# Projections over four PSUM banks, zeroing behind the last norm, and two loads and stores moved to ScalarE's queue

## The chip, the cores and the metric

One core of one Trainium2 chip runs the whole program; the other cores are idle. The metric is the device time of one execution in microseconds (us). Lower is better.

## What is computed

A two-layer model on 512 tokens of width 1024, in float32. Each layer is

```
h = rms_norm(x) ; proj = h @ w_in                       # 1024 -> 1024 + 968 + 1536 columns
mixed = concat(retention(4 heads), dsa(4 heads), dilated(8 heads))
x = x + mixed @ w_out
h = rms_norm(x) ; x = x + square(relu(h @ w_up)) @ w_down   # 1024 -> 4096 -> 1024
```

and a last `rms_norm` gives the output. `dsa` scores every key with an indexer of 8 heads, keeps the top keys of each query, and attends to those. `dilated` attends over three window patterns. `retention` runs in chunks of 128 tokens with a carried state.

## The kernel before

**Tiling.** Tokens are four tiles of 128 (t = 0 to 3). Every large product is made of three float32r matmuls (high·high, high·low, low·high), so each activation and each weight unit is kept as a high and a low half: ScalarE casts the high half, VectorE or GpSimd subtracts to get the low one (`prep`, L278 and L286, for weights; `norm`, L399 and L400, for activations). Weight units come through three raw buffers, loaded by DMA from SyncE's queue (`dma`, L263), into five unit buffers.

**PSUM.** Eight banks in three pools: `mm` has 2 (projections, output product, up product), `at` has 4 (transposes, scores, attention output), `rt` has 2 (retention; also the second half of a `dil_v` before retention begins). A new tile of a pool waits until the readers of the oldest one are done.

**Start.** `start()` loads a row of norm weights and two halves of token tile 2, spreads the row over 128 partitions with two matmuls (L1075), and then `norm` runs for tiles 2, 3, 0, 1. A norm squares the tile on ScalarE (L361), adds two sums on VectorE (L364), raises to the power -0.5 on GpSimd (L368, which gives the factor `r`), scales on VectorE (L387 and L389), transposes on TensorE (L352) and splits into halves (L399, L400). The first product is `token_parts` (L553, 456 columns, 96 matmuls for the four tiles).

**Attention.** The indexer (L336 with 384 columns), then top-k: 16 rounds of `max` and `match_replace` for three query tiles (L602, L603), in between the projections of the dilated heads: `proj` (L791) makes one q or k of a pair of heads in one `mm` bank, and `evac_q` and `evac_k` read it on ScalarE and on VectorE (L424, L438). `dil_v` makes the values. A head is `softmax` (L443, L444 for the scores, L462 for mask and minimum) and `attn_v` (transposes, L486 for the low half, L491). Retention steps go between the heads from head 5 on. `zeros()` (L814) fills the state `sv` and the unused halves of the two key buffers `KL` with zeros, five GpSimd instructions per layer.

**Order.** The code is handed to a scheduler that orders each engine's instructions by priorities (table `PR`) and by its own idea of when things are ready. The order on an engine is then fixed; an instruction that waits holds up all behind it on its engine.

**End.** `final(t)` scales the last norm: one half of the columns on ScalarE (L1054), the other on VectorE (L1057). Both halves are stored from SyncE's queue (L1055, L1058).

Of the kernel before, what the change touches and what calls it, by code (L numbers as in the profile page):

```python
# [21 lines left out]
ALU = mybir.AluOpType  # L22
# [3 lines left out]
P = 128  # L26
# [25 lines left out]
C = {  # L52
    'FILL': 'q1,q2 k1 k2,g0,d g1,k3,q3 r,v s0,w,s1,',
    'RET': (0, 0, 0, 0, 0, 4, 0, 3, 0, 1, 3, 1, 0),
    'TOPK': (1, 1, 0, 4, 0, 10, 0),
    'POOL_LO': ('dv', 'o', 'sq', 'rg', 'rqk', 'dq', 'dk', 'ukv'),
    'LSPLIT': 2,
    'HOLD': 6,
    'KS': ((4, 6), (0, 2)),
    'SK': 1,  # L60
# [58 lines left out]
def bc(ap, dims):  # L119

    return bass.AP(ap.tensor, ap.offset, [list(ap.ap[0])] + [list(d) for d in dims])


class Kern:
# [251 lines left out]
    def norm(self, t, wb, act, room, first=False, h0=0):  # L376

        nc = self.nc
        hn = self.t(room[0], [P, 2, S], F32, room[1])
        halves = ((0, 512), (512, 1024))[::1 - 2 * h0]  # L380
        if not first:
            c0, c1 = halves[0]
            nc.gpsimd.tensor_tensor(hn[:, h0], self.x[t][:, c0:c1], wb[:, c0:c1], op=ALU.mult)
        r = self.norm_stats(t, None, halves)
        for h in (h0, 1 - h0):
            if h == h0 and not first:
                nc.vector.tensor_scalar(hn[:, h], hn[:, h], r[:, 0:1], None, op0=ALU.mult)  # L387
            else:
                nc.vector.scalar_tensor_tensor(hn[:, h], self.x[t][:, h * 512:(h + 1) * 512], r[:, 0:1],  # L389
                                               wb[h] if first else wb[:, h * 512:(h + 1) * 512], op0=ALU.mult,  # L390
                                               op1=ALU.mult)
            ps = self.at()
            for k in range(4):
                self.tr(ps[:, k * P:(k + 1) * P], hn[:, h, k * P:(k + 1) * P])
            psv = ps.rearrange("p (k c) -> p k c", k=4)
            for g in range(2):
                dst = act[h * 2 + g]
                hi = dst[:, 0, :, t * P:(t + 1) * P]
                nc.scalar.copy(hi, psv[:, 2 * g:2 * g + 2])  # L399
                nc.vector.tensor_tensor(dst[:, 1, :, t * P:(t + 1) * P], psv[:, 2 * g:2 * g + 2], hi.bitcast(F32),  # L400
                                        op=ALU.subtract)
# [135 lines left out]
    def dil_v(self, L, act, g):  # L537
        us = [(self.unit((L, "dv", g, k)), (k, k + 1, k + 2, k + 3)) for k in (0, 4)]
        for t in range(NT):
            ps = self.mm() if t < 2 else self.rt_bank()  # L540
            self.tform(us, act, t, ps, 256)
            self.evac_dil(ps[:, 0:256], g, t)
        self.done(2)
# [238 lines left out]
    def latent_k(self, L, pr):  # L782
# [5 lines left out]
            self.done()  # L788
        return self.evac_k(ps)

    def proj(self, key, act, cols=P):  # L791
        ps = self.mm()
        self.wform(self.unit(key), act, cols, ps, cols)
        self.done()
        return ps
# [17 lines left out]

    def zeros(self):  # L814

        z = lambda o, a: self.nc.gpsimd.tensor_scalar(o, a, 0.0, 0.0, op0=ALU.mult, op1=ALU.add)
        z(self.sv.rearrange("p a c -> p (a c)"), bc(self.ident, [[0, 4], [1, P]]))
        for i in range(4):
            o = slice(64, 128) if i % 2 == 0 else slice(0, 64)
            z(self.kl[i // 2][o, i % 2, :], bc(self.ident[o], [[0, 4], [1, P]]))  # L820

    def load_x(self, t, src):
        self.x[t] = self.t(self.pv, [P, D], F32, "xv")
# [6 lines left out]
    def attention(self, L, act):  # L830
        nc = self.nc
        A = self.A
        sc = None
        self.rt = [self.t(self.pmix, [P, 2, 1024], F32, "mix") for _ in range(2)]
        self.vd, self.sg, self.ct, self.vs, self.rqk_done = {}, None, None, None, False
        self.masks = self.t(self.psc, [P, N_CST - N_C1], F32, "masks")
        nc.sync.dma_start(self.masks, A["cst"][:, N_C1:])
# [54 lines left out]
        def out_part(h, t, ks, last=False):  # L892
            ps = self.mm()
            self.tform([(self.unit((L, "o", h, k)), (k, k + 1)) for k in ks], mix, t, ps)
            self.add_x(t, h, ps)
# [4 lines left out]
        for h in range(12 + C["SK"]):  # L900
            if h < 12:
                if h == 8:
                    self.bias(sc)
                with self.prio("hs", h):
                    self.head_s(heads[h // 2], h % 2)
            for f in fill.pop(0) if fill else ():
                with self.prio("fill", f):
                    steps[f]()
            if h == 8 + C["SK"]:
                for t in range(NT):  # L910
                    self.load_x(t, self.xd if L else A["x"])
                mix = [m0, None] + self.md
            if h >= 8 + C["SK"]:
                for _ in range(C["WO"]):
                    if wo and wo[0] not in hold:
                        assert 0 not in C["KS"][0] or m0_done
                        with self.prio("wo", h):
                            out_part(*wo.pop(0), C["KS"][0])
                            if wo and wo[0] == (1, 0):
                                self.done(len(C["KS"][0]))  # L920
            if h >= C["SK"]:
                with self.prio("hv", h):
                    self.head_v(heads[(h - C["SK"]) // 2], (h - C["SK"]) % 2)
            for _ in range(C["RET"][h] if h < 13 else 0):
                with self.prio("ret", h):
                    next(rets, None)
            if h < 6:
                with self.prio("topk", h):
                    self.topk(sc, C["TOPK"][h + 1])
# [117 lines left out]
    def final(self, t, wb, pool, junk):  # L1047
        nc = self.nc
        halves = [(512, 1024), (0, 512)]
        (c0, c1), (d0, d1) = halves  # L1050
        xs = self.t(pool, [P, 512], F32, "s")
        nc.gpsimd.tensor_tensor(xs, self.x[t][:, c0:c1], wb[:, c0:c1], op=ALU.mult)
        r = self.norm_stats(t, junk, halves if t != 1 else halves[:1] + [(d0, d0 + 256), (d0 + 256, d1)])
        nc.scalar.activation(xs, xs, AF.Copy, scale=r[:, 0:1])  # L1054
        nc.sync.dma_start(self.out[t * P:(t + 1) * P, c0:c1], xs)  # L1055
        o = self.x[t][:, d0:d1]
        nc.vector.scalar_tensor_tensor(o, o, r[:, 0:1], wb[:, d0:d1], op0=ALU.mult, op1=ALU.mult)  # L1057
        nc.sync.dma_start(self.out[t * P:(t + 1) * P, d0:d1], o)  # L1058

    def start(self):  # L1060
        nc = self.nc

        row = self.t(self.pt, [P, 2 * S], F32, "PT")
        nc.sync.dma_start(row[0:1, :], self.A["attn_norm_w"][0].rearrange("(o c) -> o c", o=1))
        self.x[2] = self.t(self.pv, [P, D], F32, "xv")
        for h in range(2):
            nc.sync.dma_start(self.x[2][:, h * 512:(h + 1) * 512], self.A["x"][2 * P:3 * P, h * 512:(h + 1) * 512])
        nc.sync.dma_start(self.c[:, :N_C0], self.A["cst"][:, :N_C0])
        nc.vector.memset(self.pwr, -0.5)
        one = self.work()  # L1070
        nc.vector.memset(one, 1.0)
        wps = [self.at(), self.at()]
        wb = self.t(self.ph, [P, D], F32, "ph")
        for h in range(2):
            nc.tensor.matmul(wps[h], one[0:1, 0:P], row[0:1, h * 512:(h + 1) * 512], start=True, stop=True)  # L1075
        for h in range(2):
            nc.scalar.copy(wb[:, h * 512:(h + 1) * 512], wps[h])
        self.plan()
        self.dma()
        self.load_x(3, self.A["x"])  # L1080
        self.dma()
        self.dma()
        self.load_x(0, self.A["x"])
        self.load_x(1, self.A["x"])
        nc.sync.dma_start(self.c[:, N_C0:], self.A["cst"][:, N_C0:N_C1])
        act = self.act_tiles()
        PRE = (1, 1, 2, 1)
        for t, n in zip((2, 3, 0, 1), PRE):
            self.norm(t, wps if t == 2 else wb, act, (self.pk, "KH" if t < 2 else "Q"), t == 2)
            self.done(n)  # L1090
        return act
# [38 lines left out]
```

## Time and profile before

| | us |
|---|---|
| median of 3 runs | 1236.36 (1236.02 to 1240.37) |
| profiled execution, its own time | 1236.08 |
| its span | 1234.1 |
| TensorE matmul busy | 1207.2 (98%) |
| VectorE busy | 921.4 (75%) |
| ScalarE busy | 679.2 (55%) |
| GpSimd busy | 472.4 (38%) |

How to read it: the span is what the profiler saw between the first and the last instruction; the profiled execution took 2.0 us more than that. Busy times are sums over the whole span, so they do not tell which engine sets the pace of a stretch. In rows of a timeline the columns are start, duration, engine, line, operation, output <- input, how many instructions were merged, and in brackets the idle time before and what ended it.

### The profile page before, as it was taken

How to read it: one execution, taken by the hardware profiler on the slowest of the kernel's cores; microseconds unless marked ns; L12 is line 12 of the kernel's file. 1: busy time of each engine (PE TensorE's matmuls, PEld its weight loads, DVE VectorE, ACT ScalarE, POOL GpSimd, SP SyncE). 2: the span in 40 equal slices, each digit the busy share in tenths (PEclk: the TensorE clock that was granted, in tenths of full speed). 3: DMA queues.
4: the chain of work that ended last, by engine and by line, in shares of the span. 5: the costliest groups of instructions: out<-in, count | busy, mean ns of one | idle time of the engine just before them, and what ended most of it. 6: DMA issues, size and time to landing. Idle time of an engine off the chain costs nothing.

```text
span 1234.1 us, 16904 instructions
## 1 busy us (share of the span) xinstructions
PE 1207.2 (98%) x6116; PEld 1027.6 (83%) x6116; DVE 921.4 (75%) x1582; ACT 679.2 (55%) x1241; POOL 472.4 (38%) x461
## 2 busy tenths in 40 slices
PE   7999999999999999999999999999999999999997
PEld 5988888889888888888889888888898888888886
DVE  5599957776875966858866997687769668587596
ACT  6645758745644535535566456686465354354454
POOL 3453748553412304214224546664534032140232
PEclk9999999999999999999999999999999999999999
DMA  7432324215244061260153323231180622514201
GB/s 217 120 83 72 95 69 121 86 53 188 85 137 137 1 215 58 69 184 16 35 166 102 95 71 96 91 120 53 52 256 1 205 68 69 176 30 140 82 1 69
DMA packets 142180, 122.73 MB, mean 99 GB/s; under 512 B 6801, under 2 KB 114065, under 8 KB 142098
## 3 DMA queue, kind: packets, MB, share of 16 engines
q1 hardware_dynamic: 140178, 118.52, 31.9%
q10 hardware_dynamic: 1920, 3.15, 1.0%
q8 instruction: 48, 0.79, 0.3%
q14 instruction: 34, 0.28, 0.1%
HBM read 114.31 MB, written 4.19 MB: 96 GB/s over the span
## 4 chain that ended last, share of the span: by engine, by line
PE 85%; DVE 12%; ACT 1%; issue 1%; DMA 1%; SPq 0%; POOL 0%; POOLq 0%; DVEq 0%; ACTq 0%
PE mm L336 35%; PE mm L348 15%; PE rt L1036 14%; PE at L1036 7%; PE mm L1036 3%; DVE sc L603 3%; DVE top L602 3%; PE at L352 2%; PE at L491 2%; PE at L444 1%; PE at L443 1%; DVE ph L462 1%; PE at L336 1%; DVE Q L424 1%; DMA raw<-in_w_in_dram 1%
## 5 line engine op out<-in xcount | busy, mean ns | idle before, releaser
L336 PE MATMUL mm<-act,w 128*128 128x512 f32 (+2 forms) x2352 | 516.1, 377 | 3.1 <-DVE Q L424 3.1
L336 PEld LDWEIGHTS mm<-act,w 128*128 128x128 f32 x2352 | 424.4, 188 | 79.8 <-issue 3.9
L286 POOL TENSOR_TENSOR w<-raw,w 128x512 fp32r<-128x512 f32 (+1 forms) x124 | 160.0, 1313 | 99.2 <-ACT w L278 74.0
L278 ACT CAST w<-raw 128x1024 fp32r<-128x1024 f32 (+1 forms) x138 | 142.9, 1037 | 79.2 <-PE rt L1036 27.6
L1036 PE MATMUL rt<-w,U 128*128 128x512 f32 x768 | 183.2, 389 | 0.0
L286 DVE TENSOR_TENSOR w<-rd,w 128x1024 fp32r<-128x1024 f32 x112 | 144.7, 1304 | 50.0 <-ACT w L278 50.0
L286 DVE TENSOR_TENSOR w<-raw,w 128x1024 fp32r<-128x1024 f32 (+1 forms) x76 | 94.0, 1238 | 107.5 <-ACT w L278 107.2
L1036 PEld LDWEIGHTS rt<-w,U 128*128 128x128 f32 x768 | 144.1, 188 | 29.9
L993 POOL TENSOR_TENSOR st<-s 128x256 f32<-128x256 f32 x32 | 39.1, 1223 | 330.1 <-ACT s L982 325.3
L278 ACT CAST w<-rd 128x1024 fp32r<-128x1024 f32 x112 | 117.6, 1050 | 83.4 <-PE rt L1036 41.7
L348 PE MATMUL mm<-w,act 128*128 128x456 f32 (+2 forms) x576 | 118.4, 351 | 3.0 <-DVE act L400 1.8
L348 PEld LDWEIGHTS mm<-w,act 128*128 128x128 f32 x576 | 96.4, 189 | 15.2 <-DVE act L400 2.8
L348 PE MATMUL mm<-w,mix 128*128 128x512 f32 x384 | 97.3, 401 | 0.6 <-DVE Q L424 0.5
L1036 PE MATMUL at<-w,U 128*128 128x512 f32 (+1 forms) x396 | 97.7, 386 | 0.0
L304 DVE TENSOR_TENSOR rd<-rd,rd 128x1024 f32<-128x1024 f32 x64 | 94.3, 1473 | 0.5
L1036 PEld LDWEIGHTS at<-w,U 128*128 128x128 f32 x396 | 73.6, 188 | 15.0
L980 ACT ACTIVATE s<-mm 128x512 f32<-128x512 f32 x62 | 36.9, 595 | 84.2 <-PE mm L336 74.5
L348 PEld LDWEIGHTS mm<-w,mix 128*128 128x128 f32 x384 | 70.5, 190 | 15.2 <-DVE Q L424 0.9
L997 ACT CAST U<-st 128x1024 fp32r<-128x1024 f32 x32 | 33.7, 1054 | 80.9 <-POOL st L994 80.9
L991 POOL TENSOR_TENSOR st<-s,s 128x256 f32<-128x256 f32 x32 | 36.7, 1146 | 92.0 <-ACT s L982 92.0
L463 ACT ACTIVATE ph<-ph,sm 128x128 f32<-128x128 f32 (+1 forms) x96 | 53.9, 562 | 24.5 <-DVE sm L462 23.8
L998 DVE TENSOR_TENSOR U<-s,U 128x256 fp32r<-128x256 f32 x64 | 63.9, 998 | 0.0
(169 smaller groups left out, 1766.4 us busy)
## 6 DMA issues: line engine op xcount, KB each, us to landing
raw<-in_w_up_dram SPq DMA_DIRECT2D x64, 512.0 KB, 4.2
rd<-in_w_down_dram SPq DMA_DIRECT2D x32, 1024.0 KB, 5.1
raw<-in_w_in_dram SPq DMA_DIRECT2D x48, 512.0 KB, 3.9
raw<-in_w_out_dram SPq DMA_DIRECT2D x16, 512.0 KB, 3.9
xv<-in_x_dram SPq DMA_DIRECT2D x7, 512.0 KB, 4.8
KH<-KH ACTq DMA_DIRECT2D x24, 128.0 KB, 2.3
raw<-in_w_in_dram SPq DMA_DIRECT2D x8, 256.0 KB, 2.9
xd<-xv SPq DMA_DIRECT2D x4, 512.0 KB, 3.9
```

Source lines behind the costliest of these rows:

```text
L278: self.nc.scalar.copy(hi, src)
L286: eng.tensor_tensor(lo[:, i:i + step], src[:, i:i + step], hi[:, i:i + step].bitcast(F32), op=ALU.subtract)
L304: sub = lambda o, a, b: self.nc.vector.tensor_tensor(o, a, b, op=ALU.subtract)
L336: self.nc.tensor.matmul(ps[:cols, toks[0]:toks[1]], a, b, start=(k == 0 and j == 0), stop=(k == KB - 1 and j == 2))
L348: self.nc.tensor.matmul(ps[:, :w], a, b, start=(n == 0), stop=(n == tot - 1))
L463: nc.scalar.activation(p, p, AF.Exp, bias=a, scale=-1.0, accum_out=b)
L602: nc.vector.max(m, sc[b])
L603: nc.vector.match_replace(sc[b], m, sc[b], SENT)
L980: nc.scalar.activation(s, ps, AF.Relu)
L993: tt(st[:, 2], a[:, 0], a[:, 1], op=ALU.subtract)
L998: nc.vector.tensor_tensor(lo, src, hi.bitcast(F32), op=ALU.subtract)
L1036: nc.tensor.matmul(ps[:, c0:c1], a, w, start=(new and n == 0), stop=(n == 11), skip_group_check=True)
```

## The change

Four edits. (1) Projections and `dil_v` take their bank from a new function `bank()`: two from `mm`, two from `rt`, in turn, until retention begins in the layer; after that from `mm` alone. (2) `zeros()` multiplies by the factor `r` of the last norm and by zero, so that it can run only once that norm's factor is there; in layer 0 that is the norm of tile 1 in `start()`, in layer 1 the last norm in the MLP of layer 0. (3) The row of norm weights is loaded from ScalarE's queue. (4) The ScalarE half of each output tile is stored from ScalarE's queue. The table of priorities is as it was.

```diff
@@ norm
         r = self.norm_stats(t, None, halves)
+        self.last_r = r
@@ dil_v
-            ps = self.mm() if t < 2 else self.rt_bank()
+            ps = self.bank()
@@ before proj
+    def bank(self):
+
+        self.nbank += 1
+        return self.rt_bank() if self.nbank % 4 in (3, 0) and not self.ret_started else self.mm()
+
     def proj(self, key, act, cols=P):
-        ps = self.mm()
+        ps = self.bank()
@@ zeros
-        z = lambda o, a: self.nc.gpsimd.tensor_scalar(o, a, 0.0, 0.0, op0=ALU.mult, op1=ALU.add)
+
+        z = lambda o, a, r=slice(0, P): self.nc.gpsimd.tensor_scalar(o, a, self.last_r[r, 0:1], 0.0, op0=ALU.mult,
+                                                                     op1=ALU.mult)
@@
-            z(self.kl[i // 2][o, i % 2, :], bc(self.ident[o], [[0, 4], [1, P]]))
+            z(self.kl[i // 2][o, i % 2, :], bc(self.ident[o], [[0, 4], [1, P]]), o)
@@ attention
+        self.nbank, self.ret_started = 0, False
@@
+            self.ret_started = self.ret_started or C["RET"][h] > 0
             for _ in range(C["RET"][h] if h < 13 else 0):
@@ final
-        nc.sync.dma_start(self.out[t * P:(t + 1) * P, c0:c1], xs)
+        nc.scalar.dma_start(self.out[t * P:(t + 1) * P, c0:c1], xs)
@@ start
-        nc.sync.dma_start(row[0:1, :], self.A["attn_norm_w"][0].rearrange("(o c) -> o c", o=1))
+        nc.scalar.dma_start(row[0:1, :], self.A["attn_norm_w"][0].rearrange("(o c) -> o c", o=1))
```

The lines of the changed kernel are 1 higher from L386 on, and 6 to 10 higher from L791 on.

**First place: the start.** GpSimd before, from its first work on data (`sv` and `KL` are zeroed, `sm` are the norms' small columns, 155, 193, 229 and 270 being the factors of tiles 2, 3, 0 and 1):

```order
L816 TENSOR_SCALAR sv_301<-cst 128x512
L816 TENSOR_SCALAR KL_63_302<-cst 64x512 x2
L816 TENSOR_SCALAR KL_64_303<-cst 64x512 x2
L368 TENSOR_TENSOR sm_155<-sm_149,pw 128x1
L383 TENSOR_TENSOR Q_184<-xv_128,ph_119 128x512
L368 TENSOR_TENSOR sm_193<-sm_187,pw 128x1
```

The five zeroing instructions stood ahead of the first factor; in the change they stand behind the fourth. VectorE at the start, before (`Q_147` is the scaled tile 2, `w_177`, `w_215`, `w_251` the first weight units, `act` the transposed halves):

```order
L364 SCALAR_TENSOR_TENSOR sm_149<-sm_148 128x1
L286 TENSOR_TENSOR w_177<-raw_124,w_177 128x912
L389 SCALAR_TENSOR_TENSOR Q_147<-xv_110,sm_155,at_117 128x512
L389 SCALAR_TENSOR_TENSOR Q_147<-xv_110,sm_155,at_118 128x512
L364 SCALAR_TENSOR_TENSOR sm_187<-sm_186 128x1
L286 TENSOR_TENSOR w_215<-raw_130,w_215 128x912
L387 TENSOR_SCALAR Q_184<-Q_184,sm_193 128x512
L389 SCALAR_TENSOR_TENSOR Q_184<-xv_128,sm_193,ph_119 128x512
L400 TENSOR_TENSOR act_143<-at_158,act_143 128x2x128
L286 TENSOR_TENSOR w_251<-raw_134,w_251 128x912
L364 SCALAR_TENSOR_TENSOR sm_223<-sm_222 128x1
L400 TENSOR_TENSOR act_144<-at_158,act_144 128x2x128
```

and in the change:

```order
L364 SCALAR_TENSOR_TENSOR sm_149<-sm_148 128x1
L390 SCALAR_TENSOR_TENSOR Q_147<-xv_110,sm_155,at_117 128x512
L286 TENSOR_TENSOR w_177<-raw_124,w_177 128x912
L390 SCALAR_TENSOR_TENSOR Q_147<-xv_110,sm_155,at_118 128x512
L364 SCALAR_TENSOR_TENSOR sm_187<-sm_186 128x1
L401 TENSOR_TENSOR act_143<-at_158,act_143 128x2x128
L388 TENSOR_SCALAR Q_184<-Q_184,sm_193 128x512
L390 SCALAR_TENSOR_TENSOR Q_184<-xv_128,sm_193,ph_119 128x512
L286 TENSOR_TENSOR w_215<-raw_130,w_215 128x912
L401 TENSOR_TENSOR act_144<-at_158,act_144 128x2x128
L401 TENSOR_TENSOR act_145<-at_168,act_145 128x2x128
L286 TENSOR_TENSOR w_251<-raw_134,w_251 128x912
```

The first half of tile 2 is scaled ahead of the first weight unit, and the halves `act_143`, `act_144` and `act_145` are split ahead of the third.

**Second place: the projections after the first k, in each layer.** TensorE before (911 is q of pair 0, 947 its k, 1014 q of pair 1, `at_987` the first head's scores, 1088 q of pair 2):

```order
L336 MATMUL mm_947<-act_146,w_649 128x512 x6
L336 MATMUL mm_1014<-act_143,w_721 128x512 x6
L336 MATMUL mm_1014<-act_144,w_721 128x512 x6
L336 MATMUL mm_1014<-act_145,w_721 128x512 x6
L336 MATMUL mm_1014<-act_146,w_721 128x512 x6
L443 MATMUL at_987<-KH_978,Q_942 128x128
```

and in the change:

```order
L336 MATMUL mm_947<-act_146,w_649 128x512 x6
L336 MATMUL rt_1014<-act_143,w_721 128x512
L336 MATMUL rt_1088<-act_143,w_898 128x512 x6
L336 MATMUL rt_1088<-act_144,w_898 128x512 x6
L336 MATMUL rt_1088<-act_145,w_898 128x512 x6
L336 MATMUL rt_1088<-act_146,w_898 128x512
L336 MATMUL rt_1014<-act_143,w_721 128x512
L336 MATMUL rt_1088<-act_146,w_898 128x512
```

The two next q are made side by side in the `rt` banks, ahead of the first head's scores. VectorE, where it reads them, in the change (`sc` and `top` are the top-k's, `ph` a head's scores, `Q_1045` and `Q_1119` the two q, `KL_64_303` a key buffer):

```order
L604 MATCH_REPLACE sc_90_479<-top_304_1724,sc_90_479 128x512
L425 SCALAR_TENSOR_TENSOR Q_1045<-rt_1014,Q_1045 64x512
L425 SCALAR_TENSOR_TENSOR Q_1119<-rt_1088,Q_1119 64x512
L604 MATCH_REPLACE sc_88_477<-top_303_1721,sc_88_477 128x256
L603 MAX top_305_1727<-sc_89_478 128x8
L465 RECIPROCAL sm_1060<-sm_1060 128x1
L603 MAX top_307_1733<-sc_90_479 128x8
L465 RECIPROCAL sm_1060<-sm_1060 128x1
L603 MAX top_306_1730<-sc_88_477 128x8
L439 TENSOR_TENSOR KL_64_303<-mm_1124,KH_1155 64x512
L604 MATCH_REPLACE sc_89_478<-top_305_1727,sc_89_478 128x384
L425 SCALAR_TENSOR_TENSOR Q_1045<-rt_1014,Q_1045 64x512
```

Before, the two halves of `Q_1045` were read 32 and 33 VectorE instructions further up, the first of them within the first head's mask passes. From TensorE's product of the retention stage on, and in the whole MLP and the layer's start after it, the order is nearly or wholly as it was.

## Rows read from the trace of the kernel before

**Rows 1.** Page: span and TensorE's busy time; chain, stretch of the MLP.

```profile
span 1234.1 us, 16904 instructions
...
375.04 43.52 PE mm L336 x192
```

**Rows 2.** TensorE's waits over the whole run: us in total, times, longest.

```profile
PE at L352 <- DVE Q L389: 4.7, 1, 4.7
PE mm L336 <- DVE Q L424: 3.1, 2, 1.6
...
PE mm L348 <- DVE KL L438: 1.2, 2, 0.6
```

**Rows 3.** Timeline of the start, all engines.

```profile
0.72 0.35 SPq L1064 DMA_DIRECT2D PT<-in_attn_norm_w_dram  x1
...
1.13 0.82 SPq L1067 DMA_DIRECT2D xv<-in_x_dram  x2
...
5.23 0.16 DVE L364 SCALAR_TENSOR_TENSOR sm<-sm 128x1 f32<-128x1 f32 x1 [3.82 <-ACT P L361]
...
6.21 2.66 POOL L816 TENSOR_SCALAR KL<-cst 64x512 fp32r<-64x512 f32 x4
...
8.84 0.55 POOL L368 TENSOR_TENSOR sm<-sm,pw 128x1 f32<-128x1 f32 x1
...
9.06 1.11 DVE L286 TENSOR_TENSOR w<-raw,w 128x912 fp32r<-128x912 f32 x1 [3.67 <-ACT w L278]
...
10.09 1.40 DVE L389 SCALAR_TENSOR_TENSOR Q<-xv,sm,at 128x512 f32<-128x512 f32 x2
...
11.64 0.56 POOL L368 TENSOR_TENSOR sm<-sm,pw 128x1 f32<-128x1 f32 x1 [0.33 <-DVE sm L364]
...
12.91 0.48 DVE L387 TENSOR_SCALAR Q<-Q,sm 128x512 f32<-128x512 f32 x1
...
13.59 3.69 POOL L383 TENSOR_TENSOR KH<-xv,ph 128x512 f32<-128x512 f32 x2 [1.40 <-DMA xv<-in_x_dram]
...
13.97 0.42 DVE L400 TENSOR_TENSOR act<-at,act 128x256 fp32r<-128x256 f32 x1
...
14.30 1.85 DVE L286 TENSOR_TENSOR w<-raw,w 128x912 fp32r<-128x912 f32 x1
...
16.07 1.22 DVE L364 SCALAR_TENSOR_TENSOR sm<-sm 128x1 f32<-128x1 f32 x1
...
17.69 3.57 PE L348 MATMUL mm<-w,act 128*128 128x456 f32 x16 [1.33 <-DVE act L400]
...
34.15 0.74 POOL L657 TENSOR_TENSOR rv<-mix,rv 128x256 fp32r<-128x256 f32 x1 [13.70 <-ACT rv L656]
```

**Rows 4.** Chain that ended last: the end of the first product.

```profile
24.88 13.03 PE mm L348 x63
```

**Rows 5.** Timeline, layer 1: the zeroing beside the splits.

```profile
632.19 1.73 DVE L400 TENSOR_TENSOR act<-at,act 128x256 fp32r<-128x256 f32 x4 [0.40 <-ACT act L399]
...
633.42 2.66 POOL L816 TENSOR_SCALAR KL<-cst 64x512 fp32r<-64x512 f32 x4
```

**Rows 6.** Stretches: us, busy (instructions) of PE, PEld, DVE, ACT, POOL; clock, DMA.

```profile
57.00:146.00 89.00, 86.56 (x504) 76.32 (x503) 86.89 (x241) 52.18 (x111) 41.55 (x41) 1.00 0.31 84
```

**Rows 7.** VectorE in that stretch: two groups, and two reads of projections.

```profile
L603 DVE MATCH_REPLACE8 sc<-top,sc 128x512 f32<-128x512 f32 (+2 forms) x48 | 25.8, 543 | 0.1
L602 DVE MAX8 top<-sc 128x8 f32<-128x512 f32 (+2 forms) x48 | 24.8, 546 | 0.1
...
87.05 0.69 DVE L424 SCALAR_TENSOR_TENSOR Q<-mm,Q 64x512 fp32r<-64x512 f32 x1
...
96.84 0.68 DVE L424 SCALAR_TENSOR_TENSOR Q<-mm,Q 64x512 fp32r<-64x512 f32 x1
```

**Rows 8.** The end: SyncE's last store; and DMAs issued by ScalarE.

```profile
1230.87 0.38 SPq L1058 DMA_DIRECT2D out_dram<-xv  x1
...
L437 ACTq DMA_DIRECT2D KH<-KH x24: 468/468/536, 88.0 to 815.3; - x24
```

## The prediction

> **What bounds it now.** I read the page first: TensorE is busy 1207.2 of 1234.1 us, and 43.52 us of the chain in the MLP hold 192 matmuls, 0.227 us each, without a gap [rows 1]. There nothing but fewer matmuls would help, and the change leaves their number alone. What it can win is time in which TensorE stands: the start, the attention, the end.
>
> Second, TensorE's waits. The longest one is for the first scaled tile, 4.7 us, once; and a product (L336, L348) stands 3.1 us in two places for VectorE's L424 and 1.2 in two for L438, which read projections out of their banks [rows 2]. These are the places that edits 2 and 1 aim at.
>
> Third, the start in the timeline [rows 3]. The two sums of tile 2 are there at 5.39, but its factor (L368) is made only at 8.84: GpSimd is zeroing `sv` and `KL` until 8.87 (four of the five take 2.66, so 3.3 in all). By then the low half of the first weight unit (L286, 9.06) has come up ahead of L389 on VectorE, so the scaled tile is there from 10.09 on. TensorE runs without long gaps from 17.69 on, after a last wait of 1.33 for a split. The first product ends at 24.88 + 13.03 = 37.91 [rows 4].
>
> Fourth, the attention of layer 0 from 57 to 146 us: VectorE is busy for 86.89 of 89.00, TensorE for 86.56 [rows 6]. Both are full. The two kinds of gaps behind VectorE's reads are 1.55 and 0.6 in each layer, 2.15 together [rows 2]. The share of 75% for VectorE in the whole run hides this.
>
> **The start (edits 2 and 3).** The row leaves SyncE's queue, so what SyncE issued at 1.13 can go at 0.72, 0.41 earlier [rows 3]. ScalarE's issue of it costs about the 0.47 of its other DMA issues [rows 8] and lies ahead of its first square, which waits for the tile anyway: 0. The sums of tile 2 then come at about 5.39 - 0.41 = 4.98, and with GpSimd free the factor is ready 0.55 and a short hand-over later, at 5.6 instead of 9.39.
>
> From there by the new order on VectorE. The first half of the tile is scaled (0.7 each, 1.40 for two) at once. The first weight unit waits for ScalarE's cast as before, 9.06 - 0.41 = 8.65, and takes 1.11: 9.76. Second half of tile 2: 10.5. The first split then comes at about 11.1 instead of 13.97. The factor of tile 3 still hangs on its own load and GpSimd's product: 11.64 + 0.56 - 0.41 = 11.8; its two scalings (0.48 for L387, and 0.74) end at 12.9, the second weight unit at 14.0, and two splits of 0.4 and less at 14.3 to 14.6. So TensorE gets at 14.4 what it had at 17.69. The old order had a weight unit of 1.85 (14.30) and a sum of 1.22 (16.07) ahead of that split; both now stand behind it.
>
> At 17.69, 88 of the 96 matmuls and 16 transposes were left, and took 20.22 us to 37.91. One matmul more is left at 14.4, 13.03/63 = 0.21: 14.4 + 20.22 + 0.21 = 34.8. I add 0.5 for waits, because VectorE now runs only about half a microsecond ahead of TensorE on tiles 0 and 1 and on the third unit. **35.3 instead of 37.91: -2.6.** Nearest ends: -3.3 without these waits and with the earlier of the two splits, -0.4 if only the row's 0.41 gets through.
>
> The zeroing itself (3.3) now runs behind the fourth factor, at about 18 to 21. GpSimd's next work is L657 at 34.15 after 13.70 idle [rows 3], and the buffers are wanted after that: hidden. Without that cover it would cost 3.3. Its neighbours on VectorE are another question. What the rows show: beside GpSimd's product of two SBUF operands (L383, 13.59 to 17.28) a sum took 1.22 instead of 0.16, a weight unit 1.85 instead of 1.11 [rows 3]; beside zeroing in layer 1, four splits of a PSUM operand took 1.73, 0.43 each, no more than 0.42 elsewhere [rows 5, 3]. No row has zeroing beside a VectorE operation with two SBUF operands, so its cost is between 0 and its whole 3.3 of VectorE time. I take 0 for the sum, from the nearest row in kind, the zeroing itself [rows 5]; about five of VectorE's operations there read a tile and weights from SBUF.
>
> [...]
>
> Layer 1's zeroing (633.42) already stood behind the last norm: 0.
>
> **The banks (edit 1).** Before, q of pair 1 waits in TensorE's queue for the bank whose last reader, L424, ends at 87.05 + 0.69 = 87.7 [rows 7]. Now pairs 1 and 2 go to the two `rt` banks, which are free, so this 1.55 goes. But the reads stay on the same VectorE, which is full: of 48 `max` at 546 ns and 48 `match_replace` at 543 ns [rows 7] a part now stands ahead of them. `Q_1045` was read first at 96.84; in the new order 12 `max`, 11 `match_replace`, masks and reciprocals of the first heads lie between, and put the two reads at about 107.6 and 112.2 on the trace's spacing. The next user of that `rt` bank is the retention gate, for which TensorE is ready at about 111.8, so it waits 1.2 (to 112.2 + 0.68). A head's last split (L486) near the end of the stretch falls some 2 us later too, and takes the rest. Tallied instruction by instruction I get TensorE at +0.4 to +0.1 against before at the end of the stretch: the wait moves. **0 per layer.** Ends: -2.15 (both gaps go), and +1.6 (both new waits come in full and none goes).
>
> **The end (edit 4).** SyncE issued the last store at 1230.87, and an issue takes it 0.38 [rows 8]; the one ahead of it stood right before. With that one on ScalarE's queue the last can go 0.4 earlier, if it was the queue that held it; on the other side ScalarE's issue, 0.47, now lies between its last squares. **-0.1**, from -0.4 to +0.3.
>
> **Sum.** 1236.08 - 2.6 + 0 - 0.1 = 1233.4. The profiled execution lies 0.3 under the median of 1236.36, so the two need no other base. A difference of 0.5%, 6.2 us, is about what a measurement of this kernel can tell from no change: under 1230.2 is faster, over 1242.5 slower.
>
> **Rivals.**
>
> A, *the banks bring their whole gain.* If VectorE's order has slack that I do not see (it is idle 2.1 of 89 us), the gaps go in both layers: 1233.4 - 3.1 - 1.2 = 1229.1. For it: q of pairs 1 and 2 side by side keep TensorE fed across the wait. Against: VectorE ends its top-k no earlier, and TensorE needs the last mask. 0.20.
>
> B, *the start gives only the row.* The zeroing stretches VectorE's scalings and splits of tiles 0 and 1 by 2 of its 3.3, or the third weight unit, now behind three splits, comes late for TensorE by as much: 1236.08 - 0.4 - 0.1 = 1235.6. For it: the stretched sum and unit beside L383 [rows 3]. Against: the splits, which read PSUM, were not stretched [rows 5]. 0.15.
>
> C, *slower than before.* The late read of `Q_1045` and `Q_1119` makes TensorE wait one top-k round more: three `max` and three `match_replace`, 3 x (0.546 + 0.543) = 3.3, at the gate and again in layer 1. 1233.4 + 6.6 = 1240.0. It decides against the change from (2.6 + 0.1)/2 = 1.35 us per layer on. For it: nothing in the new order lets the reads overtake the top-k. Against: TensorE has two more products ready ahead of that wait. 0.10.
>
> **How the numbers follow.** The forecast has 0.55: its own range is 1231.5 to 1235.3, from the start's near end and +0.4 per layer of the banks with a microsecond for the end and for the clock (TensorE's granted clock in the stretch read is 1.00, 2.4 GHz [rows 6], and may fall for a few microseconds elsewhere). To leave out no more than 2 in 10 the range takes in A in large part and B, and the lower half of C: 1228.3 to 1238.5. Faster by over 0.5%: A but for its upper part, and a little of the forecast's own tail, 0.22. Slower by over 0.5%: C with its price doubled, 0.05. Within: 0.73.
>
> **What would show it.** After the change: L368 of tile 2 at 5.6; the first product's end at 35.3 (B: 37.5); TensorE's wait of 1.55 before q of pair 1 gone and a new one of about 1.2 before the retention gate (A: none; C: 4 and more); VectorE still full up to 143; the last two stores issued by two engines, with less than 0.4 between them; VectorE's scalings at 18 to 21 at 0.74 (B: over 1). I am wrong if the first product's end moves by less than 1 us, or if TensorE's gaps in the attention change by over 1.5 us per layer.

## The result and the profile after

| | before | after |
|---|---|---|
| median | 1237.26 us (4 runs, 1236.02 to 1240.37) | 1248.30 us (4 runs, 1247.13 to 1250.91) |
| ratio, 95% interval | | 1.0094, 1.0073 to 1.0116 |
| span of the profiled execution | 1234.1 us | 1248.9 us |

The change makes the kernel 11 us slower, 9 to 14 by the interval. The forecast was 1233.4, and the range ended at 1238.5.

The page of the changed kernel, its span, its busy times and the row of TensorE's granted clock (40 slices of the span, in tenths; 9 is 90% or more):

```profile
span 1248.9 us, 16865 instructions
PE 1219.2 (98%) x6116; PEld 1034.1 (83%) x6116; DVE 919.6 (74%) x1582; ACT 679.5 (54%) x1241; POOL 476.3 (38%) x461
PEclk9999999989999999999999999999899999999999
```

TensorE has the same 6116 matmuls and is busy 12 us longer. That is no new work: two slices of the clock row, one in each layer, show an 8. Some 7 of the 12 lie there (5.1 and 2.2); the rest is spread in shares of under 1 us.

**Where the time came from.** Both orders hold the same matmuls, and they run level again at many places: the same work, by lines, tiles and shapes, is done ahead of the matmul with that number (counted from 0). The start of that matmul, after minus before, is read from the two traces; the steps between are these:

| TensorE's matmuls | what lies there | step, us |
|---|---|---|
| 0 to 300 | start of layer 0 | -2.6 |
| 300 to 747 | projections, top-k | +1.4 |
| 747 to 1219 | other heads, retention | +0.9 |
| 1219 to 1394 | last two heads | +2.1 |
| 1394 to 1500 | end of the last head, output product, at a lower clock | +5.4 |
| 1500 to 3400 | MLP, start of layer 1 | +0.2 |
| 3400 to 3797, 3797 to 4269 | the same two stretches in layer 1 | +1.5, +0.9 |
| 4269 to 4444 | last two heads | +2.1 |
| 4444 to 4500 | end of the last head, output product | +2.8 |
| 4500 to the end | MLP, end | +0.1 |

They sum to 14.8, the difference of the profiled executions (1248.9 against 1234.1); the one profiled after is the slowest of its four.

**The start** went as forecast. The timeline of the changed kernel answers to [rows 3, 4]:

```profile
5.42 0.56 POOL L368 TENSOR_TENSOR sm<-sm,pw 128x1 f32<-128x1 f32 x1 [4.99 <-DVE sm L364]
...
6.01 0.75 DVE L390 SCALAR_TENSOR_TENSOR Q<-xv,sm,at 128x512 f32<-128x512 f32 x1 [0.67 <-POOL sm L368]
...
10.58 0.42 DVE L401 TENSOR_TENSOR act<-at,act 128x256 fp32r<-128x256 f32 x1
...
13.24 0.74 DVE L401 TENSOR_TENSOR act<-at,act 128x256 fp32r<-128x256 f32 x2
...
14.94 4.17 PE L348 MATMUL mm<-w,act 128*128 128x456 f32 x19
...
35.18 3.11 PE L336 MATMUL mm<-act,w 128*128 128x384 f32 x17
```

The factor of tile 2 is there at 6.0 (forecast 5.6), the split that TensorE waited for at 14.0 (14.3 to 14.6), and the indexer's first product starts at 35.18 where it was 37.75: -2.6. In the kernel before:

```profile
37.75 1.57 PE L336 MATMUL mm<-act,w 128*128 128x384 f32 x8
```

**The projections.** The waits of TensorE that answer to [rows 2], and the places of the four new ones in layer 0:

```profile
PE at L492 <- ACT PT L486: 4.4, 6, 1.1
...
PE rt L348 <- DVE P L646: 2.9, 2, 1.5
...
PE rt L336 <- DVE Q L425: 1.0, 2, 0.6
```

```profile
109.89 3.65 PE L336 MATMUL rt<-act,w 128*128 128x512 f32 x15 [0.40 <-DVE Q L425]
...
128.38 0.51 PE L492 MATMUL at<-PT,xv 128*128 128x512 f32 x1 [1.10 <-ACT PT L486]
...
129.91 0.33 PE L444 MATMUL at<-KH,Q 128*128 128x128 f32 x1 [0.36 <-DVE PT L487]
...
132.61 2.65 PE L348 MATMUL rt<-w,act 128*128 128x256 f32 x20 [1.46 <-DVE P L646]
```

The 3.1 and the 1.2 of [rows 2] are gone. In their place, 3.3 us in layer 0: 0.40 before the gate (0.64 in layer 1), 1.10 and 0.36 in the first pair's second head, 1.46 before the last tile of the second `dil_v`, whose `rt` bank is the gate's and is read by VectorE's L646. All four end on VectorE's queue, also the 1.10 that the profile puts down to ScalarE:

```profile
126.82 0.15 DVE L465 RECIPROCAL sm<-sm 128x1 f32<-128x1 f32 x1
...
127.00 0.72 ACT L469 ACTIVATE ph<-ph,sm 128x512 f32<-128x512 f32 x1 [1.95 <-DVE sm L465]
127.74 0.59 ACT L486 CAST PT<-at 128x512 fp32r<-128x512 f32 x1
```

The split L486 stands behind the scaling L469 on ScalarE, and that waits 1.95 for a reciprocal among the top-k's instructions.

**The last two heads** are the place that the prediction did not look at. From matmul 764 on, behind the projections, the order departs again and again from that of the kernel before (the +0.9 of the table), and from 1219 to 1394 throughout. TensorE in the changed kernel, layer 0:

```profile
251.70 3.13 PE L348 MATMUL mm<-w,mix 128*128 128x512 f32 x13
...
259.77 0.69 PE L492 MATMUL at<-PT,vs 128*128 128x384 f32 x4
260.30 0.29 PE L352 MATMUL at<-cst,ph 128*128 128x128 f32 x1
261.42 0.38 PE L492 MATMUL at<-PT,vs 128*128 128x256 f32 x1 [0.82 <-ACT PT L486]
...
265.91 0.44 PE L492 MATMUL at<-PT,vs 128*128 128x384 f32 x1 [0.28 <-ACT PT L486]
266.80 1.31 PE L492 MATMUL at<-PT,vs 128*128 128x384 f32 x5 [0.45 <-DVE PT L487]
...
269.60 0.32 PE L674 MATMUL rt<-rT 64*128 64x128 f32 x1 [0.68 <-ACT rT L665]
270.46 1.59 PE L674 MATMUL rt<-rT 64*128 64x128 f32 x11 [0.53 <-DVE rT L666]
```

The same place in the kernel of the first experiment, whose order here is that of the kernel before:

```profile
253.33 0.97 PE L492 MATMUL at<-PT,vs 128*128 128x384 f32 x6
254.14 3.11 PE L348 MATMUL mm<-w,mix 128*128 128x512 f32 x13
...
260.31 0.97 PE L492 MATMUL at<-PT,vs 128*128 128x384 f32 x6
...
262.79 0.32 PE L674 MATMUL rt<-rT 64*128 64x128 f32 x1 [0.67 <-ACT rT L665]
263.64 1.35 PE L674 MATMUL rt<-rT 64*128 64x128 f32 x11 [0.53 <-DVE rT L666]
```

There 13 products of the output (L348, 3.11 us) stand between one group of attention products and the next, and TensorE does not wait for the splits. In the change they were made earlier, at 251.70, and the splits are waited for in the open. The two waits of the retention step (0.68, 0.53) are in both.

Windows of the changed kernel, of these waits and of the ten microseconds behind them (us; busy of PE, PEld, DVE, ACT, POOL; granted clock; DMA):

```profile
254.00:272.00 18.00, 14.86 (x83) 11.85 (x81) 11.74 (x25) 7.91 (x15) 8.20 (x8) 0.97 0.33 88
272.00:282.00 10.00, 10.00 (x32) 8.40 (x32) 4.57 (x11) 2.19 (x6) 3.87 (x5) 0.55 0.00 1
```

TensorE stood for 3.1 of 18 us, and then its granted clock fell to 0.50 for 10.2 us (by windows of 1 us, from 270.9 to 281). The stretch with it is 5.4 longer than before, more than the 2.1 of the two heads. Layer 1 has 6.8 us at 0.50 behind the same waits. The kernel before had 3.4 in layer 1 and none in layer 0.

### The profile page after: what moved, and what is told of

The parts are those of the page before. It is cut to its first block, busy times and chain, and to the rows that moved or that the text cites. A ratio compares the mean times of both kernels' runs of the same rounds, so it can differ in the third digit from the quotient of the medians.

```text
span 1248.9 us, 16865 instructions
## 1 busy us (share of the span) xinstructions
PE 1219.2 (98%) x6116; PEld 1034.1 (83%) x6116; DVE 919.6 (74%) x1582; ACT 679.5 (54%) x1241; POOL 476.3 (38%) x461
## 5 line engine op out<-in xcount | busy, mean ns | idle before, releaser
L336 PE MATMUL mm<-act,w 128*128 128x512 f32 (+2 forms) x2160 | 472.1, 376 | 0.0
L336 PEld LDWEIGHTS mm<-act,w 128*128 128x128 f32 x2160 | 389.1, 188 | 69.3
L286 DVE TENSOR_TENSOR w<-raw,w 128x1024 fp32r<-128x1024 f32 (+1 forms) x76 | 93.9, 1236 | 102.7 <-ACT w L278 102.5
L348 PE MATMUL mm<-w,act 128*128 128x456 f32 (+2 forms) x576 | 118.8, 353 | 0.5 <-DVE act L401 0.5
L348 PEld LDWEIGHTS mm<-w,act 128*128 128x128 f32 x576 | 97.3, 190 | 12.6 <-DVE act L401 1.1
L348 PE MATMUL mm<-w,mix 128*128 128x512 f32 x384 | 101.4, 412 | 1.6 <-DVE Q L425 1.1
L348 PEld LDWEIGHTS mm<-w,mix 128*128 128x128 f32 x384 | 73.1, 198 | 16.9 <-PE rt L352 1.5
```

The source lines that it names most:

```text
L286: eng.tensor_tensor(lo[:, i:i + step], src[:, i:i + step], hi[:, i:i + step].bitcast(F32), op=ALU.subtract)
L336: self.nc.tensor.matmul(ps[:cols, toks[0]:toks[1]], a, b, start=(k == 0 and j == 0), stop=(k == KB - 1 and j == 2))
L348: self.nc.tensor.matmul(ps[:, :w], a, b, start=(n == 0), stop=(n == tot - 1))
```

## The experiments

Letters stand for the theories that the expectations name. T is that the loss sits in the order that edit 1 gives TensorE. S puts it on the earlier start, E on the early part of edit 1 (the projections) with all else following from it. Of the early part, V says that the moved reads wait in VectorE's full queue, O that TensorE's own order costs. A and B are the prediction's.

The bank calls are numbered in each layer: the second `dil_v`'s tiles are 12 to 15, q of pairs 1 and 2 are 7 and 8, the gates 11 and 16.

**1. `no_banks`: the change without edit 1.**

```diff
-        return self.rt_bank() if self.nbank % 4 in (3, 0) and not self.ret_started else self.mm()
+        return self.mm()
@@ dil_v
-            ps = self.bank()
+            ps = self.mm() if t < 2 else self.rt_bank()
```

> The change without its edit on the banks (edit 1); zeroing, row and output store as in the change. TensorE's order is then that of the change at the start and that of the kernel before everywhere else. Theory T (the loss sits in the order that the bank edit gives TensorE): the start's 2.6 us stay, the rest is as before, 1236.1 - 2.6 + 0.1 = 1233.6, and no stretch at a granted clock of 0.50 in layer 0. Rival S (it is the start, 2.6 us earlier, that brings loads and GpSimd's zeroing into other work, and the clock falls for that): 1245 or more, with the clock at 0.50 near 270 us.

1233.28 (11 runs) against 1236.20 for before beside it, ratio 0.9973 (0.9959 to 0.9987). The first product ends 2.5 us earlier, and the clock is at 0.50 for 3.4 us in layer 0, none in layer 1, as much as before in sum. T's "no stretch at a granted clock of 0.50 in layer 0" was a miss, but its time is right and S's is not: the start does not bring the loss. The trace is also 1.2 us shorter than before in the projections of each layer, at which no edit aimed; the last section has the cause, and it bears on what is compared with this kernel below.

**2. `banks_alone`: the kernel before with edit 1 alone** (edits 2 to 4 of the diff undone).

> The kernel before with the edit on the banks alone. Theory T: before plus 1.4 us in each layer where the projections are made, plus 0.7 us and some 2 us of new waits later in the attention of each layer, plus 4 to 8 us for the clock in the two layers together: 1247 to 1253. Rival S: 1236 plus 2.8, so 1239, and no fall of the clock in layer 0.

1251.91, ratio 1.0129 (1.0110 to 1.0147). The whole loss is edit 1's. The clock was at 0.50 for 17.1 us in three stretches.

**3 and 4. The early and the late part of edit 1 apart.** Two choices of banks give TensorE the order of the change in one part and of the kernel before in the other.

```diff
-        return self.rt_bank() if self.nbank % 4 in (3, 0) and not self.ret_started else self.mm()
+        return self.rt_bank() if self.nbank in (3, 4, 7, 8, 11, 14, 15) else self.mm()
```

> The change, but only q of pairs 1 and 2 and the first gate go to the rt banks; the second dil_v and the second gate take theirs as before. TensorE's order is that of the change up to about 115 us and that of the kernel before from 141 us on. Theory T: the early part costs at most 1.4 us per layer, the late part nothing: 1233.6 to 1236.5, no 0.50 clock in layer 0. Rival E (the early part, where VectorE reads the two q late, is what costs, and all later waits follow from it): 1245 or more.

With `(3, 4, 14, 15, 16)` in that line:

> The change, but only the second gate goes to an rt bank that did not before. TensorE's order is that of the kernel before up to about 140 us and that of the change from there on. Theory T: the early gain and loss are gone, the late loss stays: 1233.6 plus 2 x 0.7, plus 2 x 2 for waits before the last heads' products, plus 4 to 8 for the clock: 1243 to 1247, with the clock at 0.50 for some microseconds near 275 and 890 us. Rival E: 1233 to 1235.

The early part: 1238.47 (12 runs), 1.0013 (0.9996 to 1.0030), 5.2 above `no_banks`. The late part: 1241.85, 1.0058 (1.0037 to 1.0079), 8.6 above `no_banks`. T had the late part in the right place, with a time a microsecond under its range, and the early one too small; E had them the wrong way round. The late waits of `rt_g1`, and a window of 1 us behind them, with the clock at 0.50 (columns as in the windows above):

```profile
259.11 0.39 PE L492 MATMUL at<-PT,vs 128*128 128x256 f32 x1 [0.82 <-ACT PT L486]
...
264.49 1.30 PE L492 MATMUL at<-PT,vs 128*128 128x384 f32 x5 [0.48 <-DVE PT L487]
```

```profile
269.00:270.00 1.00, 1.00 (x5) 0.88 (x5) 0.71 (x3) 0.40 (x1) 0.00 (x0) 0.50 0.00 0
```

The late part comes from one gate in another bank, some 120 us ahead of the place where the time is lost: TensorE's order departs a little from about 141 us on, and the output products come earlier. That the scheduler's idea of when things are ready does this is argued, not shown. Not all of the 8.6 is the late order's: `rt_g1` is as long as before in the projections, where `no_banks` is 1.2 shorter in each layer, so in the traces 2.3 of it are that. In the early part my 1.4 per layer was the waits alone; here the clock fell behind them as well (6.8 us at 0.50 from 130.6 to 137.4, and 3.4 from 741.6; 6.8 more in layer 1 behind the retention waits). The changed kernel, with the same order of TensorE in this stretch and the same first waits, had no such fall. A window of 1 us there, `rt_q1_q2_g0` first, then the changed kernel:

```profile
131.00:132.00 1.00, 0.60 (x2) 0.00 (x0) 1.00 (x3) 0.37 (x1) 0.93 (x1) 0.50 0.00 0
```

```profile
131.00:132.00 1.00, 0.15 (x1) 0.00 (x0) 1.00 (x3) 0.37 (x1) 0.87 (x1) 1.00 0.00 0
```

**5 and 6. Half of the top-k.**

```diff
-    'TOPK': (1, 1, 0, 4, 0, 10, 0),
+    'TOPK': (1, 1, 0, 4, 0, 2, 0),
```

with the `mm` banks of experiment 1, and with the `rt` banks of experiment 3.

> Top-k with 8 rounds in place of 16 (so fewer keys are kept and the output differs), projections from the mm banks as before, start and end as in the change. VectorE has about 26 us less to do in each layer between 73 and 146 us. It is the base for the next kernel; theory V (VectorE's top-k queue is what the moved reads wait for) and rival O (TensorE's own order is what costs) both expect some 1230 to 1234 here, with the wait of TensorE before q of pair 1 (about 0.6 to 1.7 us) still there, since the first rounds are still there.

> The same 8 rounds, with q of pairs 1 and 2 and the first gate on the rt banks. The late order of TensorE is the same in both from 203 us on. With 16 rounds these banks cost 5 us (1238.5 against 1233.3). Theory V: with the queue on VectorE half as long the cost goes, and the wait before q of pair 1 is gone: 0 to 3 us faster than half_topk_mm. Rival O: 3 to 5 us slower than half_topk_mm, as with 16 rounds.

1242.31 (10 runs) and 1243.20 (10 runs). The same stretch of both as in [rows 6], first with the `mm` banks:

```profile
57.00:146.00 89.00, 87.44 (x506) 77.14 (x506) 63.76 (x169) 52.39 (x111) 45.67 (x45) 1.00 0.28 80
```

```profile
57.00:146.00 89.00, 88.48 (x514) 77.92 (x513) 65.22 (x178) 54.64 (x117) 46.23 (x47) 1.00 0.29 82
```

With VectorE at 64 of 89 us the `rt` banks gain in this stretch: TensorE is busy 1.0 us more, where the change with its full VectorE was 0.9 under before (85.67 against 86.56). Between matmuls 300 and 747, and in the same place of layer 1, the `rt` banks are 0.7 us shorter, the second time with the meeting of the last section fallen alike in both (1.43). So V holds for the stretch. In the whole time neither theory does: 0.9 slower, which the spread of the two does not tell from nothing, and in the second's trace new waits (0.73 and 0.66) come up from 156 to 159 us, with 3.4 us at 0.50 behind them.

The larger surprise is the first: some 25 us less on VectorE in each layer (half of the 50.6 of [rows 7]), and the kernel is 9 us slower than `no_banks`. Its order turned late in the attention, too, into that of the change, with the same waits (0.82, 0.24, 0.28, 0.45 and 0.14 us from 258 to 265) and 6.8 us at 0.50 behind them in each layer. So the bad order is not the banks' own; another edit ahead of it sets it off as well.

**7 and 8. The start's two edits alone.** Edit 2 alone, and edit 3 alone, on the kernel before.

> The kernel before with the edit on the zeroing alone. By the prediction's sum: the start gains 2.6 less the row's 0.4, so the first product ends at 35.7 to 35.8 in place of 37.9, and the time is 2.2 us under before, 1234.0. Rival B (zeroing beside VectorE's work gives it back): the first product ends at 37.5 and the time stays within 0.5 us of before.

> The kernel before with the load of the norm weights' row on ScalarE's queue alone. By the prediction's sum: all loads 0.4 us earlier, the first product ends at 37.5 in place of 37.9, the rest as before. Rival: GpSimd's zeroing still holds the first factor until 9.4 us, so nothing of it arrives: 37.9.

`zeros_alone` 1234.66 against 1237.50, ratio 0.9976 (0.9958 to 0.9993); the first product ends 2.5 us earlier. In its trace the whole gains only 1.2: 1.4 is lost again in layer 1's output product, with two new waits (0.58 and 0.21). `row_alone` is one run (1239.58): the first product ends 0.3 earlier, with the clock at 0.50 for 13.7 us in the order of the kernel before. The indexer's product, which starts where the first one ends, in each:

```profile
35.28 2.94 PE L336 MATMUL mm<-act,w 128*128 128x384 f32 x16
```

```profile
37.45 2.78 PE L336 MATMUL mm<-act,w 128*128 128x384 f32 x15
```

The row is worth 0.3 by itself and about 0.1 once the zeroing is out of the way.

**9 and 10. One bank moved.** `(3, 4, 8, 14, 15)` and `(3, 4, 11, 14, 15)` in the line of experiment 3.

> The change, but q of pair 2 alone goes to an rt bank that it did not use before. TensorE makes it ahead of q of pair 1, and from 141 us on its order is nearly that of the kernel before. Theory V (a product moved ahead of a busy VectorE leaves its read in the same queue): the wait before q of pair 1 goes, but the read of q of pair 1 is late as in the change and the waits come back at the first heads' scores: 1233 to 1237, against 1233.3 with no banks changed. Rival A (the bank's whole gain): 1233.3 - 2 x 1.1 = 1231 or less.

> The change, but the first gate alone goes to an rt bank. The reads of the two q are where they were before, and from 141 us on TensorE's order is that of the kernel before. Theory V: nothing is late that was not, so within 1.5 us of no_banks, 1232 to 1235. Rival E (any gate on an rt bank stands in the way of retention's banks): 1236 or more.

`rt_q2` 1232.75 (12 runs), 0.9978 (0.9967 to 0.9989), the same as `no_banks`: the wait before q of pair 1 is gone in its trace, and one for L425 has come before the gate:

```profile
108.73 1.62 PE L336 MATMUL mm<-act,w 128*128 128x512 f32 x6 [0.88 <-DVE Q L425]
```

That is V's kind of wait, though not at the first heads' scores, where V had it. Against A the time says little: in `no_banks` the wait was only 0.42 in each layer, so A had 0.8 to gain, not 2.2. `rt_g0` 1244.89, 1.0069 (1.0051 to 1.0087): a miss of V, which looked at reads that move and not at what is left behind. The rival in its expectation, also called E there, has the number (1236 or more), but its mechanism, a gate in the way of retention's banks, is not what the trace shows. The waits of `rt_g0`:

```profile
PE at L444 <- DVE PT L487: 3.5, 4, 1.4
PE mm L336 <- DVE Q L425: 3.1, 2, 1.6
...
PE at L444 <- DVE sm L463: 2.7, 2, 1.4
```

and the windows of this place and behind it:

```profile
120.00:129.00 9.00, 7.37 (x52) 6.31 (x51) 8.97 (x31) 7.62 (x17) 3.41 (x4) 1.00 0.06 15
129.00:136.00 7.00, 5.33 (x19) 4.49 (x20) 6.94 (x24) 3.64 (x11) 4.46 (x7) 0.51 0.55 169
```

With the gate begun at 90.75 us, nothing stands between the second head's transposes and the next scores, which wait for VectorE (busy 8.97 of 9.00 us); then the clock falls, in both layers. It is the late part's pattern at another place. In the last two heads its order is that of the kernel before.

**11. `no_banks_no_store`: experiment 1 without edit 4.**

> The change without the edit on the banks and without the store on ScalarE's queue: zeroing and row alone. By the prediction's sum the store is worth 0.1: 1233.4 where no_banks had 1233.3. From the ends of the traces so far (7.75 to 7.82 us from TensorE's last matmuls to the end of the span with ScalarE's store, 7.64 to 7.70 with SyncE's) it is the other way, and this one is 0.1 faster. A rival, that the store on ScalarE's queue overlaps the last writes, would show 0.4 us and more against this kernel.

1232.72 (12 runs), ratio 0.9972 (0.9958 to 0.9986): no difference that can be told from `no_banks`. From the start of TensorE's matmul 6110 to the end of the span it is 7.68 to 7.70 us in the five traces with SyncE's store, and 7.76 to 7.78 in the eight with ScalarE's. This kernel, `no_banks` and `rt_q2` are 0.2 to 0.3% under the kernel before and further under the changed one, and can't be told from each other.

These two profiles also price the clock. The kernels differ in the store alone; `no_banks` was at 0.50 for 3.4 us and this one for 13.7, and their spans are 1229.3 and 1233.1: 3.8 us for 10.2, an estimated 0.4 each, with TensorE's order one and the same. That is of the size of the 4.4 us between the fastest and the slowest run of `no_banks`.

## Why the prediction was wrong

**The step that failed** is the one on the banks, "0 per layer", in two places.

First in its own stretch. The tally had TensorE at +0.4 to +0.1 at its end; +1.4 was measured in layer 0 and +1.5 in layer 1, near the bound of +1.6. The mechanism was right: VectorE is the full engine [rows 6], the reads stay on it, and the wait comes back. The gate's wait was sized 1.2 and measured 0.40 and 0.64, and the late split was there too (0.36). What the tally missed is that an `rt` bank of the gate goes to the second `dil_v` next (1.46), and that ScalarE's queue hands VectorE's lateness on (1.10).

Second, and larger, the tally stopped at 146 us. The prediction, and the part ahead of it on the order, took TensorE's order behind the retention stage as nearly the old one. It was not: in the last two heads the output products had moved ahead of the attention products that they used to cover. The two heads are 2.1 us longer in each layer, and the stretches at the lower clock behind them 5.4 and 2.8. `rt_g1`, whose order in the later attention is that of the change, shows both; `rt_q1_q2_g0`, with the early one alone, does not have them there.

**The rivals.** A (the whole gain) is out: in the changed kernel both old waits are gone, and the stretch is 1.4 and 1.5 longer all the same. B is out: the start brought 2.6, and no VectorE operation beside the zeroing took over 0.1 more than it does elsewhere, see the last section. C had the sign, and one place of its mechanism (the gate, L425), but its price of a top-k round at that read is not what happened.

**The clock** stood in the prediction as a microsecond of noise. No run shows the frequency that stands there: the traces show the granted clock as a share of full speed, 1.00 in that stretch and 0.50 behind the waits, and in the changed kernel a 128x512 matmul took 389 ns on average from 380 to 400 us, at 1.00, and 640 from 271.5 to 280.5, at 0.50. By the runs, TensorE's waits in a row were followed by a granted clock of 0.50 in 10 of 10 layers with the late order (3.4 to 10.2 us, 6.5 on average) and in 10 of 16 with the order of the kernel before (3.4 on average over the 16), in which the two retention waits stand alone. That the waits are what brings it down fits all of these, and the falls at earlier places (`rt_q1_q2_g0`, `rt_g0`, `banks_alone`, `half_topk_rt`) stand behind waits as well. But the early waits of the changed kernel brought none in either layer, and no run took the waits away and kept the rest: it is a correlation, its cause is not shown, and how long the clock stays at 0.50 differs between traces of the same order (3.4 us in `no_banks`, 13.7 in `no_banks_no_store`).

**What was right.** The start: -2.6 forecast and measured, by the steps named, with `zeros_alone` at 2.5 of it. The split between its two edits was off: the row had 0.4 and is worth 0.1 to 0.3. That `no_banks` came out at 1233.28, beside the forecast of 1233.4, is in part luck, since its trace has the 1.2 us per layer of the last section, which the sum did not. The store: nothing that can be measured; the traces have it 0.1 the other way. The zeroing of layer 1: nothing, since `zeros_alone` is 2.5 ahead of before at the start of layer 0 and still 2.5 at the end of layer 1's attention.

## What to carry to other kernels

Where a scheduler sets the order, compare the whole order of the engine that bounds the kernel before costing an edit: the time was lost 120 us behind the edit, by products that were no longer there to cover a wait. A freed buffer lets work run early, and work run early is cover spent; ask what stood behind it. Read the granted clock behind a series of short waits of TensorE before pricing them by their sum: behind the late order's it was 0.50 in 10 of 10 layers.

## What the runs showed of the hardware

**Zeroing beside VectorE.** GpSimd's instruction took longer here, not VectorE's. The first `KL` instruction of the changed kernel and VectorE beside it:

```profile
19.14 2.56 POOL L823 TENSOR_SCALAR KL<-cst,sm 64x512 fp32r<-64x512 f32 x1
```

```profile
19.07 0.48 DVE L388 TENSOR_SCALAR KH<-KH,sm 128x512 f32<-128x512 f32 x1
19.46 0.75 DVE L390 SCALAR_TENSOR_TENSOR KH<-xv,sm,ph 128x512 f32<-128x512 f32 x1
20.12 1.10 DVE L286 TENSOR_TENSOR w<-raw,w 128x912 fp32r<-128x912 f32 x1
21.14 0.42 DVE L401 TENSOR_TENSOR act<-at,act 128x256 fp32r<-128x256 f32 x1
```

It took 2.56 where it takes 0.7 (four took 2.66 before, while VectorE was idle [rows 3]), and ended 0.56 after VectorE had come to L401, which reads a PSUM tile (21.14). VectorE's three operations on SBUF, back to back, ran at their usual 0.48, 0.75 and 1.10. The four took 5.75 in all, and GpSimd was not needed until 31.65. What holds GpSimd's instruction up is not shown; the prediction's rival B had the loss on VectorE.

**A tie worth 1.15 us.** The wait that edit 1 was to remove was mostly such a meeting. In the kernel before, VectorE's last mask operation ahead of the top-k (L593) and a weight unit on GpSimd start together:

```profile
75.45 1.42 DVE L593 SCALAR_TENSOR_TENSOR sc<-masks,sc 128x128 f32<-128x128 f32 x1
```

```profile
75.43 2.59 POOL L286 TENSOR_TENSOR w<-raw,w 128x512 fp32r<-128x512 f32 x2
```

and in `no_banks`:

```profile
72.89 0.28 DVE L594 SCALAR_TENSOR_TENSOR sc<-masks,sc 128x128 f32<-128x128 f32 x1
```

```profile
72.87 2.71 POOL L286 TENSOR_TENSOR w<-raw,w 128x512 fp32r<-128x512 f32 x2
```

1.42 or 0.28, with the same 0.02 between the starts. It was 0.28 in both layers of `no_banks`, `rt_q2` and `no_banks_no_store`, and in one layer each of `banks_alone`, `rt_q1_q2_g0` and `half_topk_rt`, whose other layer had 1.42 or 1.43; so it can come out either way in one execution; what decides it is not shown. With 0.28, VectorE's top-k ran 1.15 earlier. In the eight kernels whose order up to q of pair 1 is that of the kernel before, TensorE's wait there is 0.42 in the layers with 0.28, and 1.56 to 1.58 in all others. No edit aimed at this, so a comparison with `no_banks` has up to 2.3 us of it in its difference.
